# Holding the first store of a rotate kernel until nearly all loads have landed, with the last load split to make that possible

## The chip, the cores and the metric

One core of one Trainium2 chip. The metric is the device time of one execution in microseconds (us), taken over several runs; all runs in this text are in the fast state, and the granted clock is 1.00 in every profile. The change is judged against 2%. The span of a profile is 1.5 to 2 us shorter than the time of its run.

## The reference

```python
def setup_inputs():
    return {"x": np.random.randn(32, 3, 256, 256).astype(np.float32)}

def reference(x):
    return np.rot90(x, k=-1, axes=(-2, -1)).astype(np.float32)
```

96 images of 256 x 256 floats are turned by a quarter. 25.17 MB are read and 25.17 MB written. There is no arithmetic: the work is to load, transpose on VectorE, and store.

## The kernel before

The images are cut into twelve slabs of 2 MB. Each has its own SBUF tile `units[n]` of 128 partitions x 2 x 2048 floats. Slab n is turned into the tile of slab n-1, which has been consumed by then; slab 0 is turned into PSUM and copied out by ScalarE at the end.

```python
    for n in range(n_slabs):                       # all loads, on the SyncE queue
        if n == last:
            nc.sync.dma_start(out=units[n], in_=ld8_v[n])            # 2 MB, rows of 8 KB
            continue
        for i in range(I):
            if n == 0:
                nc.sync.dma_start(out=units[n][:, i], in_=ld8_v[n][:, i])
            else:                                  # 64 partitions: the even ones, then the odd ones
                nc.sync.dma_start(out=units[n][i::I].rearrange("p i f -> p (i f)"), in_=ld16_v[n, i])

    for n in range(n_slabs):
        t_in, t_out = units[n], units[n - 1] if n else turned0
        ...                                        # two VectorE transposes, t_out <- t_in
        if n == 1:                                 # first stores, same queue
            nc.sync.dma_start(out=st_v[n][:, 0, :W], in_=t_out[:, 0, :W])    # 128 KB
            nc.sync.dma_start(out=st_v[n][:, 0, W:], in_=t_out[:, 0, W:])    # 896 KB
            nc.sync.dma_start(out=st_v[n][:, 1], in_=t_out[:, 1])            # 1 MB
        elif n:
            nc.sync.dma_start(out=st_v[n], in_=t_out)                        # 2 MB
    ...                                            # ScalarE copies slab 0 out of PSUM, last store
```

Of the kernel before, what the change touches and what calls it, by code (L numbers as in the profile page):

```python
# [1 line left out]

# [4 lines left out]




@with_exitstack
def kernel(
    ctx: ExitStack,
    tc: tile.TileContext,
    x: bass.AP,
    out: bass.AP,
):

















    nc = tc.nc
    fp32 = mybir.dt.float32

    B, C, H, W = x.shape
    P = nc.NUM_PARTITIONS  # L40
    RI, RO = 16, 8
    K = H // RI
    I = 2
    Q = P // (K * I)
    n_slabs = B * C // (Q * I)
    last = n_slabs - 1
    F = RO * W

    rows_in = x.rearrange("b c h w -> (b c h) w")
    rows_out = out.rearrange("b c h w -> (b c h) w")  # L50
    ld8_v = rows_in.rearrange("(n i p r) w -> n p i (r w)", i=I, p=P, r=RO)
    ld16_v = rows_in.rearrange("(n i m r) w -> n i m (r w)", i=I, m=Q * K, r=RI)
    st_v = rows_out.rearrange("(n i p c) w -> n p i (c w)", i=I, p=P, c=RO)

    pools = [ctx.enter_context(tc.tile_pool(name=f"unit{u}", bufs=1)) for u in range(n_slabs)]
    units = [pool.tile([P, I, F], fp32, name=f"u{u}") for u, pool in enumerate(pools)]
    psum = ctx.enter_context(tc.tile_pool(name="psum", bufs=1, space=bass.MemoryType.PSUM))
    turned0 = psum.tile([P, I, F], fp32, name="turned0")

    for n in range(n_slabs):  # L60
        if n == last:
            nc.sync.dma_start(out=units[n], in_=ld8_v[n])
            continue
        for i in range(I):
            if n == 0:
                nc.sync.dma_start(out=units[n][:, i], in_=ld8_v[n][:, i])  # L66
            else:
# [4 lines that stand above are left out]
        if n in (0, last):  # L72
            for i in range(I):
                src = t_in[:, i].rearrange("p (r g c) -> p c r g", r=RO, c=RO)
                dst = t_out[:, i].rearrange("p (c g r) -> p c r g", c=RO, r=RO)
                nc.vector.transpose(out=dst[:, :, ::-1, ::-1], in_=src)  # L76
        else:
            src = t_in.rearrange("p i f -> p (i f)").rearrange("p (r g c) -> p c r g", r=RI, c=RO)
            dst = t_out.rearrange("p i (c k r) -> p c r k i", c=RO, r=RI)[:, :, ::-1, ::-1, :]
            for h in range(2):  # L80
                cs = slice(h * RO // 2, (h + 1) * RO // 2)
                nc.vector.transpose(out=dst[:, cs], in_=src[:, cs])  # L82

        if n == 1:
            nc.sync.dma_start(out=st_v[n][:, 0, :W], in_=t_out[:, 0, :W])
            nc.sync.dma_start(out=st_v[n][:, 0, W:], in_=t_out[:, 0, W:])
            nc.sync.dma_start(out=st_v[n][:, 1], in_=t_out[:, 1])
        elif n:
            nc.sync.dma_start(out=st_v[n], in_=t_out)  # L89

    for i in range(I):
        nc.scalar.copy(out=units[last][:, i], in_=turned0[:, i])  # L92
    nc.sync.dma_start(out=st_v[0], in_=units[last])


# [1 line left out]
_INS = ['x']  # L97
_OUTS = [((32, 3, 256, 256), 'float32')]


# [23 lines left out]
```

## Time and profile before

| | |
|---|---|
| time, median of 3 runs | 124.06 us (123.96 to 124.23) |
| span of the profile | 122.2 us |
| DMA engines busy | 97.8% of the span |
| VectorE busy | 93.3 us, ends at 99.2 us |
| first store issued, landed | 42.28 us, 62.93 us |

The prediction below shows the page, the windows and the timeline.

(A packet is one piece of a transfer, here 8 KB of one partition. Every transfer also has 16 completion packets of 4 bytes, 592 for the 37 transfers here. I read them as one for each of the 16 DMA engines, which tells when each was done.)

### The profile page before, as it was taken

The page shows a single profiled execution, that of the slowest core. Times are in us where ns is not written, and L with a number is a line of the kernel's source. Part 1 is how long each engine was busy: PE and PEld are TensorE (multiplying, and loading weights), DVE is VectorE, ACT ScalarE, POOL GpSimd, SP SyncE. Part 2 cuts the span into 40 slices and gives each one's busy share as a digit, 9 for nine tenths or more (in the row PEclk, how much of TensorE's full clock was granted, in tenths as well). Part 3 has the DMA queues.
Part 4 walks back from the last instruction along what each step waited for, and adds up shares of the span by engine and source line. Part 5 has one row for each costly group of instructions (what it writes and reads, how often), then busy time and mean ns, then how long its engine had stood idle before and what let it go on. Part 6 is the DMA issues. An engine that isn't in the chain of part 4 may idle for free.

```text
span 122.2 us, 134 instructions
## 1 busy us (share of the span) xinstructions
DVE 93.3 (76%) x24; ACT 5.0 (4%) x3; POOL 0.2 (0%) x4
## 2 busy tenths in 40 slices
DVE  0299999999999999999999999999999940000000
ACT  0000000000000000000040000000000651000000
POOL 0000000000000000000000000000000000000000
DMA  3999999999999999999999999999999999999993
GB/s 88 429 432 434 440 440 429 429 429 429 429 429 429 429 429 424 434 424 408 370 414 428 426 429 429 429 429 429 429 429 429 424 429 429 429 429 426 429 429 166
DMA packets 5584, 50.33 MB, mean 412 GB/s; under 512 B 592, under 2 KB 720, under 8 KB 848
## 3 DMA queue, kind: packets, MB, share of 16 engines
q1 hardware_dynamic: 5584, 50.33, 97.8%
HBM read 25.17 MB, written 25.17 MB: 412 GB/s over the span
## 4 chain that ended last, share of the span: by engine, by line
DMA 57%; DVE 13%; issue 7%; DVEq 3%; ACT 2%; SPq 1%
DMA u<-in_x_dram 39%; DMA out_dram<-u 18%; DVE u L82 10%; DVE u L76 3%; DVEq L119 3%; ACT u L92 2%; SPq L66 1%; SPq L89 0%
## 5 line engine op out<-in xcount | busy, mean ns | idle before, releaser
L82 DVE STREAM_TRANSPOSE u<-u 128x2048 f32<-128x2048 f32 x20 | 78.0, 3948 | 0.3
L76 DVE STREAM_TRANSPOSE turned<-u 128x2048 f32<-128x2048 f32 x2 | 7.6, 3828 | 5.5 <-DMA u<-in_x_dram 5.5
L76 DVE STREAM_TRANSPOSE u<-u 128x2048 f32<-128x2048 f32 x2 | 7.8, 3953 | 0.0
L92 ACT COPY u<-turned 128x2048 f32<-128x2048 f32 x2 | 3.7, 1866 | 33.8 <-DVE u L76 33.8
L92 ACT ACT_TABLE_LOAD x1 | 1.3, 1283 | 62.4 <-DMA u<-in_x_dram 62.4
L108 POOL MEMSET const-bfloat16-1.0<- 128x1 bf16 x1 | 0.1, 102 | 0.0
L108 POOL MEMSET const-uint8-127<- 128x1 uint8 x1 | 0.1, 102 | 0.0
L108 POOL MEMSET const-float32-0.0<- 128x1 f32 x1 | 0.1, 99 | 0.2 <-issue 0.2
L108 POOL MEMSET const-float32-1.0<- 128x1 f32 x1 | 0.1, 99 | 0.0
## 6 DMA issues: line engine op xcount, KB each, us to landing
u<-in_x_dram SPq DMA_DIRECT2D x22, 1024.0 KB, 19.6
out_dram<-u SPq DMA_DIRECT2D x11, 2048.0 KB, 25.0
u<-in_x_dram SPq DMA_DIRECT2D x1, 2048.0 KB, 22.5
out_dram<-u SPq DMA_DIRECT2D x1, 1024.0 KB, 20.2
out_dram<-u SPq DMA_DIRECT2D x1, 896.0 KB, 20.2
out_dram<-u SPq DMA_DIRECT2D x1, 128.0 KB, 20.6
```

The costliest lines, as they stand in the source:

```text
L66: nc.sync.dma_start(out=units[n][:, i], in_=ld8_v[n][:, i])
L76: nc.vector.transpose(out=dst[:, :, ::-1, ::-1], in_=src)
L82: nc.vector.transpose(out=dst[:, cs], in_=src[:, cs])
L92: nc.scalar.copy(out=units[last][:, i], in_=turned0[:, i])
L108: nc = _bacc.Bacc("TRN2", target_bir_lowering=False, num_devices=1)
L119: with _tile.TileContext(nc) as tc:
```

## The change

Its intent: keep stores out of the DMA queue while loads run, and leave just so many loads in flight (0.75 MB) that the latency of the first store is covered. To have something to wait on near the end, the last 2 MB load is cut in three.

```diff
+    M = P // 4
...
         if n == last:
-            nc.sync.dma_start(out=units[n], in_=ld8_v[n])
+            nc.sync.dma_start(out=units[n][:, 0], in_=ld8_v[n][:, 0])
+            near_end = nc.sync.dma_start(out=units[n][:M, 1], in_=ld8_v[n][:M, 1])
+            nc.sync.dma_start(out=units[n][M:, 1], in_=ld8_v[n][M:, 1])
             continue
...
         if n == 1:
-            nc.sync.dma_start(out=st_v[n][:, 0, :W], in_=t_out[:, 0, :W])
+            first = nc.sync.dma_start(out=st_v[n][:, 0, :W], in_=t_out[:, 0, :W])
+            tc.add_manual_dep(first.ins, near_end.ins.name, mybir.DependencyInfo(
+                mybir.DependencyClass.Sync, mybir.DependencyReason.DATA), reason="stores after loads")
```

## The prediction

> **What bounds the kernel now.** I read the page first (busy shares and the forty slices), then the chain of work that ended last, then the SyncE queue's waits and the timeline, then narrow windows and the packet records around the middle of the run, where the change acts. First the page of the kernel before:
>
> ```profile
> DVE 93.3 (76%) x24; ACT 5.0 (4%) x3; POOL 0.2 (0%) x4
> DVE  0299999999999999999999999999999940000000
> ...
> DMA  3999999999999999999999999999999999999993
> GB/s 88 429 432 434 440 440 429 429 429 429 429 429 429 429 429 424 434 424 408 370 414 428 426 429 429 429 429 429 429 429 429 424 429 429 429 429 426 429 429 166
> ...
> q1 hardware_dynamic: 5584, 50.33, 97.8%
> ...
> out_dram<-u SPq DMA_DIRECT2D x1, 128.0 KB, 20.6
> ```
>
> The 16 DMA engines are busy for 97.8% of the 122.2 us span, and the rate stands at 429 GB/s while they load and while they store. VectorE has stopped by slice 33. So bytes set the end: 50.33 MB at 429 GB/s are 117.3 us; the rest, 4.9 us, is a start of about 2.4 us, a tail of about 1.4 us after the last packet (120.83 in the packet records), and about 0.5 us lost in the one dip, slices 18 to 21 (408, 370, 414). The dip is where loads give way to stores. The windows there (columns: stretch, length, busy time of DVE, ACT and POOL, clock, DMA share, GB/s):
>
> ```profile
> 57.00:58.00 1.00, 1.00 (x1) 0.00 (x0) 0.00 (x0) 1.00 1.00 418
> 58.00:59.00 1.00, 1.00 (x1) 0.00 (x0) 0.00 (x0) 1.00 1.06 442
> 59.00:60.00 1.00, 1.00 (x1) 0.00 (x0) 0.00 (x0) 1.00 1.06 385
> 60.00:61.00 1.00, 0.96 (x2) 0.00 (x0) 0.00 (x0) 1.00 0.86 270
> 61.00:62.00 1.00, 1.00 (x1) 0.00 (x0) 0.00 (x0) 1.00 1.00 397
> 62.00:63.00 1.00, 1.00 (x1) 0.64 (x1) 0.00 (x0) 1.00 1.05 434
> ```
>
> Between 59 and 62 us the rate falls to 385, 270, 397: (429-385)+(429-270)+(429-397) = 235 KB short, or 0.55 us. The engines are not idle there. The 8 KB packets of the last load, 0.309 us each earlier on, take 0.45 to 0.77 us in some thirty cases; the first 1 KB packet of a store is recorded only at 61.36 us.
>
> The timeline shows when each store is handed to the queue (columns: start, duration, engine, line, operation):
>
> ```profile
> 1.64 36.15 SPq L68 DMA_DIRECT2D u<-in_x_dram  x20
> ...
> 13.09 78.34 DVE L82 STREAM_TRANSPOSE u<-u 128x2048 f32<-128x2048 f32 x20
> 39.77 0.39 SPq L62 DMA_DIRECT2D u<-in_x_dram  x1
> 42.28 0.36 SPq L85 DMA_DIRECT2D out_dram<-u  x1
> ...
> 101.15 0.37 SPq L93 DMA_DIRECT2D out_dram<-u  x1
> ```
>
> The first store is issued at 42.28 us but lands 20.6 us later, at 62.9: it lies behind about 8 MB of loads in the same queue. The last store is issued at 101.15 and lands at 121.18, so even there the queue has 20 us of work in hand. VectorE and ScalarE are nowhere near the path, though the printed chain follows the ScalarE copies at the end; that chain puts the time to the issue, not to the queue ahead of it.
>
> [...] each 1 MB load takes 19.56 us to land because eight lie in the queue (8 x 2.445 us)[...]. [...] the first load is issued at 0.73 us, its first packets start at 1.74 to 1.83 on eight engines and at 2.41 to 2.53 on the other eight, so 1.0 and 1.7 us; I use these. [...]
>
> **The change part by part.**
>
> 1. The last 2 MB load becomes three: 1 MB, 0.25 MB (32 partitions), 0.75 MB (96 partitions). Bytes are the same, and packets stay 8 KB. Two more issues of about 0.4 us on SyncE lie under a queue of some 8 MB: nothing on the path. Each engine gets two more completion packets of 0.009 us: 0.02 us.
>
> 2. The first store gets a second wait. The order of the issues doesn't change, as the built kernel's instruction listing confirms: all loads, then the same stores. The eight completion semaphores that the DMAs share rotate by two, so some stores wait for another predecessor; every such predecessor is a load or a store eight places earlier, done by then. In the listing the only new wait that can end last is the one on the 32-partition load.
>
> 3. The stores which used to be queued from 42 to 62 us (six issues by 57 us) are held and issued in one burst. VectorE goes on: it writes each turned slab into a buffer whose input was consumed already, and no transpose waits for a store. By 60 us slabs 1 to 5 are turned (13.09 + 7.83 us per slab puts slab 5 at 52.2 and slab 6 at 60.1), which is some 10 MB or 24 us of stores. After that a slab comes every 7.8 us and drains in 4.9, as before; the backlog at 101 us is still about 19 us. So nothing later in the run moves except by what happens at the turn.
>
> 4. The turn itself. The last 1 MB load before the final one has its per-engine completion packets at 56.21 to 56.46. The 1.25 MB ahead of the trigger are 10 packets per engine: 10 x 0.309 + 0.02 = 3.11 us, so 59.32 to 59.57; a load's semaphore counts 0.31 us after that packet (first load: packets at 4.85 to 5.11, semaphore 5.21 to 5.47): the last at about 59.9. SyncE passes a satisfied wait in 0.07 us, so the store is issued at 59.95 and its packets start 1.0 us later on half of the engines (60.95) and 1.7 us later on the other half (61.65). Meanwhile the 0.75 MB are 6 packets per engine, 1.86 us: loads end at 61.18 to 61.45. So half of the engines meet no gap, and half a gap of 0.2 to 0.45 us. The next stores follow at 0.41 us per issue; the first holds 8 packets of 0.046 us = 0.37 us per engine, so the queue doesn't run dry again by more than 0.05 us.
>
> 5. What the hold removes. Before, the loads end per engine between 61.36 and about 61.93 instead of the 61.16 to 61.41 that 16 packets of 0.309 us from 56.21 to 56.46 would give: the fastest engine lost 0.2 us, the slowest 0.5. That spread of 0.57 us is still there at the end, where the completion packets of the last store lie at 120.21 to 120.82, 0.61 us apart. The slowest engine ends the run. I suppose, without proof, that the slow load packets come from store descriptors standing right behind them. If so, the hold takes most of it away: the slowest engine goes from loads to stores at about 61.65 (its gap) instead of 61.93: -0.3 us. I count two thirds, since stores still reach half of the engines 0.2 to 0.5 us before the loads end.
>
> Sum: +0.02 (completion packets) + 0.05 (issue spacing) - 0.3 (turn), so -0.2 to -0.25: 124.06 becomes about 123.8 us.
>
> **The rivals.** (a) The wait makes a bubble: the latency is not covered by 0.75 MB. If the slow half of the engines starts 2.5 us after the landing rather than 1.7, or the landing itself is delayed because reads are slow at the turn, all of the dip (0.5) returns as idle time, and 0.5 to 1 us more: 124.3 to 125. For it: the 1.0 and 1.7 us come from one cold issue only. Against: a store reads its source from SBUF, and the first load's slow start contains an HBM read (its first packets took about 1 us instead of 0.31). (b) The slow packets belong to the end of the loads and not to the stores behind: then the dip stays and the gap partly adds: 124.1 to 124.6. For it: store packets are recorded only after the slow ones. Against: nothing like it at earlier borders between loads. (c) Reads and writes in one stretch cost much, and parting them wins over 1%: against it speaks [...] 429 GB/s on both sides of the dip; 0.55 us is all there is to win: 123.5. (d) The lost prequeueing starves the tail: against it the 20 us backlog at the last issue; even a gap of 1 us at the turn leaves VectorE and ScalarE off the path.
>
> **Range and chances.** The best case is the dip gone and no gap: 123.5; runs differ by 0.1 to 0.2 us, so the low end is 123.2. The bad case (a) gives 125 at the extreme; I put the high end at 124.7. A move of 2% is 2.5 us. On the gain side there are 0.55 us; on the loss side all engines would have to stand idle for 2.5 us in the middle, while a whole cold start takes 1.7. Hence 1% for faster, 97% for the same, 2% for slower.
>
> **What would show it.** In the changed kernel: the first store issued near 60 us in place of 42, then stores about 0.4 us apart until slab 5's; the 59 to 62 us windows at 385 or above in the first, and a dip that lies after 61 us, if at all, and shows as a low DMA share rather than slow packets; the first store landing within 3 us of its issue in place of 20.6; VectorE still ending near 99.2 and the last store still issued near 101; completion packets of the last store at 0.3 to 0.5 us apart. Step 4 is wrong if a hole of over 0.5 us with a DMA share under a half stands at 61 to 62. Step 5 is wrong if load packets of 0.45 us and over are still there before 61 us. The whole is wrong if rates away from the turn change, or if a later wait of SyncE for a store's semaphore holds a ready slab back.

+0.02, +0.05 and -0.3 us, together -0.2 to -0.25 us, are estimates from numbers of the trace. That the split adds nothing beyond its 0.02 us stands unproved.

## More of the kernel before

One more view of the kernel before is wanted for the comparison: the windows of the long store stretch (columns: stretch, its length, busy us and instructions of DVE, ACT and POOL, granted clock, share of the DMA engines, GB/s).

```profile
66.00:80.00 14.00, 13.93 (x5) 0.00 (x0) 0.00 (x0) 1.00 1.01 429
80.00:100.00 20.00, 19.16 (x5) 2.61 (x2) 0.00 (x0) 1.00 1.01 428
100.00:119.00 19.00, 0.00 (x0) 1.12 (x1) 0.00 (x0) 1.00 1.01 429
```

The rate does not move over 53 us. Behind it stands something that I looked at only after the result: in the packet records, every single 8 KB store packet from 66 to 119 us took exactly 309 ns.

## The result, and the profile after

The changed kernel takes 125.80 us in the median (125.41 to 126.25, 6 runs), the kernel before 124.09 (123.96 to 124.23, 6 runs). The ratio is 1.014, with a 95% interval of 1.0115 to 1.0165. Ratios here are the mean time of one kernel's fast runs over that of the other's from the same rounds, so not quite the ratio of the medians. It is inside the 2% band, as forecast, but on the other side of zero: 1.7 us slower, where 0.2 us faster was predicted, and outside the range. The profiled run was the slowest of the six (126.25), so the traces differ by 2.3 us of span where the medians differ by 1.7.

From the page of the changed kernel, the rate in forty slices and the issue of the first store (line, engine, operation, KB, us from issue to landing):

```profile
GB/s 90 427 453 427 427 437 432 421 437 432 421 432 432 427 427 427 442 421 395 219 357 428 429 416 429 413 424 419 421 416 421 421 421 419 421 421 421 421 421 213
...
out_dram<-u SPq DMA_DIRECT2D x1, 128.0 KB, 2.9
```

Two things have changed in the first line. The dip at slices 18 to 20 is far deeper (395, 219, 357 for 408, 370, 414). And to the right of it the rate sinks within some five slices to about 421, where it was 429, and stays there: not a stall, but a lower rate to the end. The second line shows that the wait does what it was meant to do: the first store lands 2.9 us after its issue, no longer 20.6.

The windows of the changed kernel (columns as above):

```profile
58.00:59.00 1.00, 1.00 (x1) 0.00 (x0) 0.00 (x0) 1.00 1.11 410
59.00:60.00 1.00, 1.00 (x1) 0.00 (x0) 0.00 (x0) 1.00 1.03 213
60.00:61.00 1.00, 0.96 (x2) 0.81 (x1) 0.00 (x0) 1.00 1.06 205
61.00:62.00 1.00, 1.00 (x1) 0.47 (x1) 0.00 (x0) 1.00 0.97 262
62.00:63.00 1.00, 1.00 (x1) 0.00 (x0) 0.00 (x0) 1.00 0.93 238
63.00:64.00 1.00, 1.00 (x1) 0.00 (x0) 0.00 (x0) 1.00 1.03 363
66.00:80.00 14.00, 13.93 (x5) 0.00 (x0) 0.00 (x0) 1.00 1.01 424
80.00:100.00 20.00, 19.36 (x5) 2.40 (x2) 0.00 (x0) 1.00 1.01 420
100.00:119.00 19.00, 0.00 (x0) 1.33 (x1) 0.00 (x0) 1.00 1.01 419
```

From 59 to 63 us about half the rate is missing (205 to 262 GB/s) with a DMA share of about 1 (0.93 to 1.06). So this is no idle queue: the engines are busy with packets that take long, in the packet records 0.43 to 0.76 us for every 8 KB packet in this stretch. That is not the bubble of the prediction's rival (a), which would show a low share (hold_whole below has one, of 0.06 to 0.12).

The timeline says when SyncE acted (start, duration, engine, line, operation):

```profile
42.46 0.35 SPq L65 DMA_DIRECT2D u<-in_x_dram  x1
44.91 0.32 SPq L66 DMA_DIRECT2D u<-in_x_dram  x1
...
61.84 0.37 SPq L89 DMA_DIRECT2D out_dram<-u  x1
62.30 0.38 SPq L92 DMA_DIRECT2D out_dram<-u  x1
...
101.36 0.37 SPq L99 DMA_DIRECT2D out_dram<-u  x1
```

The first store goes out at 61.84 us, not at 59.95, because the 32-partition load on which it waits (L65) landed only at 61.75. The last store is issued at 101.36, 0.2 us later than before, with 22 us of queue ahead of it: nothing in VectorE or ScalarE has become a bound.

To tell the turn from the stores I use two numbers from the landings. The third store (the 1 MB one) lands at 67.36 us before and 69.15 after: +1.8 us at the turn. From there to the last landing 53.82 us pass before and 54.44 after: +0.6 us in the store stream. Together they are the 2.4 us by which the last store lands later (123.59 for 121.18).

A landing is the last of a transfer's 16 semaphore counts (66.67 to 67.36 us for the third store before), so that of the slowest engine, and this hides part of the second loss. By the completion packets the engines end the third store 0.61 us apart before and the last store 0.61 us apart as well; after, 0.70 and then 0.26 us. In the mean of the engines, the third store ends 1.7 us later (68.28 for 66.59) and the way from there to the last store takes 0.9 us longer (54.82 for 53.90).

### The profile page after: what moved, and what is told of

Read it like the earlier page. It is cut to its first block, busy times and chain, and to the rows that moved or that the text cites. A ratio compares the mean times of both kernels' runs of the same rounds, so it can differ in the third digit from the quotient of the medians.

```text
span 124.5 us, 137 instructions
## 1 busy us (share of the span) xinstructions
DVE 93.3 (75%) x24; ACT 5.0 (4%) x3; POOL 0.2 (0%) x4
## 3 DMA queue, kind: packets, MB, share of 16 engines
q1 hardware_dynamic: 5616, 50.33, 98.1%
## 4 chain that ended last, share of the span: by engine, by line
DMA 51%; DVE 13%; issue 10%; DVEq 6%; ACT 1%
DMA u<-in_x_dram 51%; DVE u L86 13%; DVEq L125 6%; ACT u L98 1%; DVE u L80 0%
```

## The experiments

The first theory (A) after reading the trace: the 32- and 96-partition loads are slow in themselves, because of the partitions that each of them writes. That was a supposition, and why partitions should matter is shown by no trace or run here. The rival (B): the hold itself costs. Twelve kernels were run in three batches of four, each with five rounds against the kernel before on the same chip. All gave correct results. The chip differs from batch to batch, so ratios of one batch can be compared more closely than ratios of two.

A table first, to which the paragraphs refer. "Excess" is the time by which the 8 KB packets between 56 and 64 us exceeded 309 ns, summed and divided by the 16 engines. "Third store" and "to last" are the two landing numbers from above. The last column has the mean duration of the 8 KB store packets from 66 to 75 us and from 100 to 119 us. All but median and ratio are from the profiled run.

| kernel | excess, us | third store, us | to last, us | 8 KB store packet, ns | median, us | ratio to before |
|---|---|---|---|---|---|---|
| before | 0.41 | 67.36 | 53.82 | 309.0, 309.0 | 124.09 | |
| changed | 1.97 | 69.15 | 54.44 | 311.9, 315.2 | 125.80 | 1.0140 |
| split_only | 2.21 | 69.38 | 53.77 | 309.0, 309.0 | 125.72 | 1.0117 |
| hold_columns | (2 and 6 KB packets) | 68.01 | 54.99 | 318.6, 315.2 | 125.37 | 1.0095 |
| columns_only | (2 and 6 KB packets) | 68.37 | 53.80 | 309.0, 309.0 | 124.89 | 1.0054 |
| hold_whole | 0.07 | 68.81 | 54.97 | 319.7, 315.1 | 126.58 | 1.0191 |
| halves_hold | 0.07 | 66.96 | 54.73 | 311.0, 315.1 | 124.37 | 1.0019 |
| halves_only | 0.74 | 67.72 | 53.85 | 309.0, 309.0 | 124.01 | 0.9999 |
| block64_only | 2.38 | 69.39 | 53.78 | 309.0, 309.0 | 125.92 | 1.0149 |
| stride64_only | 0.37 | 67.26 | 53.85 | 309.0, 309.0 | 123.78 | 0.9972 |
| drain_mid | 0.30 | 67.15 | 56.09 | 309.0, 315.0 | 126.27 | 1.0187 |
| hold_2mb | 0.28 | 67.15 | 53.80 | 309.0, 309.0 | 123.70 | 0.9979 |
| hold_1p5mb | 0.06 | 67.03 | 53.76 | 309.0, 309.3 | 123.45 | 0.9960 |
| stride_both | 0.35 | 67.32 | 53.89 | 309.0, 309.0 | 123.95 | 0.9996 |

The kernel before had medians of 124.29, 124.06 and 123.92 us in the three batches. Measured by the 2% of this text, hold_whole and drain_mid are unclear, since their intervals reach over 1.02, and all others count as the same; what is said of smaller differences rests on their intervals. In the mean of the engines, "to last" is 53.90 us in every kernel with 309.0 ns at both places, 53.93 in hold_1p5mb, 54.68 in halves_hold, 54.82 in the changed kernel and 55.05 in hold_columns and hold_whole.

### The split without the hold (split_only)

```diff
  # against the changed kernel
-            tc.add_manual_dep(first.ins, near_end.ins.name, ...)
```

> The three-way split of the last load (128, 32 and 96 partitions) stays, the hold on the first store is taken away. Theory A (the 32- and 96-partition loads themselves run slow[...]): as slow as the changed kernel, 125.3 to 126.2 us, and windows of 200 to 270 GB/s from 59 us on, with the 8 KB load packets at 0.45 to 0.75 us. Theory B (the hold costs: the stores come late, the queue runs dry or the stores come in a burst): back to the kernel before, 123.9 to 124.3 us. Theory C (half of each): about 125.0.

Measured: 125.72 us (125.23 to 125.94), ratio 1.0117 (1.0094 to 1.014). Its windows:

```profile
59.00:60.00 1.00, 1.00 (x1) 0.00 (x0) 0.00 (x0) 1.00 1.13 229
60.00:61.00 1.00, 0.96 (x2) 0.73 (x1) 0.00 (x0) 1.00 0.97 156
61.00:62.00 1.00, 1.00 (x1) 0.56 (x1) 0.00 (x0) 1.00 0.97 238
62.00:63.00 1.00, 1.00 (x1) 0.00 (x0) 0.00 (x0) 1.00 0.90 225
...
100.00:119.00 19.00, 0.00 (x0) 1.21 (x1) 0.00 (x0) 1.00 1.01 428
```

The deep dip is there without any hold, so theory A holds for the turn: most of the loss is the split. But the store packets are back at exactly 309 ns, which means that the second loss, in the stores, comes with the hold. I had not expected that division.

### The hold with a split along the row, and its control (hold_columns, columns_only)

```diff
  # hold_columns, against the changed kernel; columns_only is the same without the hold
-            near_end = nc.sync.dma_start(out=units[n][:M, 1], in_=ld8_v[n][:M, 1])
-            nc.sync.dma_start(out=units[n][M:, 1], in_=ld8_v[n][M:, 1])
+            near_end = nc.sync.dma_start(out=units[n][:, 1, :F // 4], in_=ld8_v[n][:, 1, :F // 4])
+            nc.sync.dma_start(out=units[n][:, 1, F // 4:], in_=ld8_v[n][:, 1, F // 4:])
```

> The hold stays, at the same 0.25 MB and 0.75 MB, but the last megabyte is split along the row (128 partitions x 2 KB, then 128 x 6 KB) and no longer by partitions. Theory A: the loads run at full rate up to the turn; 123.5 to 124.4 us, and the prediction's sum for the hold (-0.2 us) gets its first clean test. Theory B: as slow as the changed kernel, 125.3 to 126.2 us.

> The control of the run before it: the column split, no hold. Theories A and B both expect the kernel before within 0.2 us (123.9 to 124.3). If it is slower by 0.5 us or more, one more split of any kind costs[...].

Measured: 125.37 us with the hold (ratio 1.0095, 1.0074 to 1.0115) and 124.89 without (1.0054, 1.0036 to 1.0073). Both are misses. The control is 0.6 us slower than the kernel before, so this was not a clean way to split: its 2 KB packets took 0.08 us at best and up to 0.73 us, while the 6 KB packets behind them ran at 0.234 us, the rate of the 8 KB ones. All 128 partitions take part, so theory A doesn't explain it. The stores behind explain part: with the stores held, the same packets took 0.38 us at most, and their sum per engine was 1.19 us for 1.60, where 8 packets at 0.084 are 0.67. The rest I did not follow further. By my own words of expectation one more split of any kind costs, which left theory A in doubt, and it needed a better test (below).

The pair is still of use, as the hold is the only difference within it. With the hold the third store lands 0.36 us earlier (68.01 for 68.37), which has the sign and about the size of the saving at the turn that the prediction counted on, and then the stores take 1.2 us longer (54.99 for 53.80) with packets of 315 ns and more. A saving and a larger loss.

### The last load whole, all stores held until it has landed (hold_whole)

```diff
  # against the kernel before
-            nc.sync.dma_start(out=units[n], in_=ld8_v[n])
+            near_end = nc.sync.dma_start(out=units[n], in_=ld8_v[n])
...
+        for st in held if n else []:      # every store of slabs 1 to 11
+            tc.add_manual_dep(st.ins, near_end.ins.name, ...)
```

> The last load is left whole, and every store is held until it has landed: no store descriptor is in the queue while loads run. If the slow load packets of 59 to 61 us come from stores right behind the loads (step 5 of the prediction), they are gone here (8 KB packets all under 0.33 us, windows at 420 to 440 until 61 us), then an idle gap of about 0.3 (landing) + 0.1 + 1.0 to 1.7 us follows: 124.9 to 125.5 us in all. If they belong to the end of the loads, the dip to 270 GB/s stays and the gap comes on top: 125.4 to 126.0.

Measured: 126.58 us, ratio 1.0191 (1.0169 to 1.0212), some 1.1 us above what was expected. Its windows:

```profile
59.00:60.00 1.00, 1.00 (x1) 0.00 (x0) 0.00 (x0) 1.00 1.04 434
60.00:61.00 1.00, 0.96 (x2) 0.00 (x0) 0.00 (x0) 1.00 0.89 369
61.00:62.00 1.00, 1.00 (x1) 0.00 (x0) 0.00 (x0) 1.00 0.12 49
62.00:63.00 1.00, 1.00 (x1) 0.95 (x1) 0.00 (x0) 1.00 0.06 23
```

Here the share is low together with the rate: this is what an empty queue looks like. No load packet exceeded 0.33 us (excess 0.07 us for 0.41). So one supposition of the prediction is confirmed in this kernel: with no stores behind the loads, the slow load packets of the dip are gone. (hold_1p5mb below adds a condition: stores that had stood there for only about 2 us did no such harm, with 0.06 us of excess.) The records also give the latency of a store into an empty queue: issued at 62.05 us, first packets on the engines at 62.90, all within some 0.15 us, so 0.85 us and not the 1.0 and 1.7 us that I took from the first load. The 1.1 us above expectation are the slower stores (54.97 for 53.82).

### Whole halves, with and without the hold (halves_hold, halves_only)

```diff
  # halves_hold, against the changed kernel; halves_only is the same without the hold
             near_end = nc.sync.dma_start(out=units[n][:, 0], in_=ld8_v[n][:, 0])
-            ... [:M, 1] and [M:, 1]
+            nc.sync.dma_start(out=units[n][:, 1], in_=ld8_v[n][:, 1])
```

> The last load is split into its two full 1 MB halves (128 partitions x 8 KB each) and the first store is held until the first half has landed, so 1 MB is left in flight. The loads use whole rows and all partitions. Theory so far, from the first four runs: the partition split costs 1.8 to 2.0 us at the turn; the hold itself saves about 0.3 us at the turn, but in all three kernels with a hold the 8 KB store packets took 315 ns on average in place of 309, which costs about 1.1 us over the stores. It expects no dip at 59 to 61 us, 315 ns packets after it, and 124.6 to 125.0 us. Rival (the slow stores come from the queue having run dry, and with 1 MB in flight it doesn't): 309 ns packets and 123.6 to 124.0 us.

> Control of the run before it: the two halves, no hold. The kernel before within 0.2 us (124.0 to 124.4), store packets of 309 ns, the dip at 59 to 61 us as before. If it is 0.5 us slower, a split of any kind costs[...].

Measured: 124.37 us with the hold (ratio 1.0019, 1.0006 to 1.0033), 124.01 without (0.9999, 0.9981 to 1.0018). The control is as fast as the kernel before, so a split by itself need not cost anything, though in its profiled run the dip was deeper (0.74 us of excess for 0.41). With the hold the dip is gone and the third store lands at 66.96 us, 0.40 us earlier than in the kernel before and 0.76 us earlier than in the control. The time is between the two expectations, and the packets say why: 80% of them were at exactly 309 ns from 66 to 75 us, 29% from 90 to 100 us, 11% from 100 to 119 us. The stores start clean and wear out. This made me suspect that the 309 ns are a state which can get lost; drain_mid below tests it.

### Which partitions, or how many (block64_only, stride64_only)

```diff
  # no hold in either; block64_only, then stride64_only
-            ... units[n][:M, 1] and units[n][M:, 1], M = 32
+            ... units[n][:64, 1] and units[n][64:, 1]
+            ... units[n][0::2, 1] and units[n][1::2, 1]
```

> No hold; the last megabyte is split into partitions 0 to 63 and 64 to 127. [...] both run at half rate: 2.45 us more than the 2.45 us of a full-rate megabyte: packets near 0.62 us throughout and 126.5 to 127.0 us, slower than the 32/96 split[...]. Rival (a DMA of fewer partitions is slow whichever they are, or one more DMA at the end costs): like the 32/96 split, about 125.7.

> No hold; the last megabyte is split into the even and the odd partitions, 64 each as in the run before it[...]. [...] full rate, 124.0 to 124.6 us. Rival (fewer partitions are slow as such): as slow as the run before it.

In both texts the figures before the word "Rival" are those of theory A. For the half rate there is a measured ground: the 32- and 96-partition loads of the changed kernel ran at 205 to 262 GB/s from 59 to 63 us, for 428 GB/s from 3 to 59 us.

Measured: 125.92 us in blocks (ratio 1.0149, 1.0134 to 1.0163) and 123.78 us interleaved (0.9972, 0.9959 to 0.9985). Two windows of the blocks, then of the interleaved parts:

```profile
60.00:61.00 1.00, 0.96 (x2) 0.80 (x1) 0.00 (x0) 1.00 1.13 238
61.00:62.00 1.00, 1.00 (x1) 0.49 (x1) 0.00 (x0) 1.00 0.91 205
```

```profile
59.00:60.00 1.00, 1.00 (x1) 0.45 (x1) 0.00 (x0) 1.00 1.05 426
60.00:61.00 1.00, 0.96 (x2) 0.84 (x1) 0.00 (x0) 1.00 1.00 320
```

Same bytes, same number of DMAs, same number of partitions, same row length; only which partitions go together differs, and 2.1 us lie between them. That tells which partitions from how many: 64 partitions in a block ran at about half rate (205 and 238 GB/s in these windows; nine in ten packets of 0.56 to 0.65 us, for 0.309), the 64 even ones at full rate (426 GB/s) until the usual dip. Why a block is slow is not shown.

The rows that are read from memory go along with the partitions, which would be a rival: a block reads 0.5 MB in one piece, the even partitions read every second row. But the kernel before had answered it. Its 20 loads of slabs 1 to 10 each bring 1 MB in one piece to the 64 even or the 64 odd partitions, and from 3 to 56 us they ran at 430 GB/s. So neither 64 partitions nor one piece of memory made these loads slow, and the profile that the prediction read showed it.

The interleaved kernel is 0.2 us below its expectation. The block's time was 0.6 us under its own, and taken alone it would have fitted the rival. The likely reason for the miss: I added the half-rate loss of 2.45 us to a run that kept the 0.41 us dip, while slow loads take the place of that dip. 2.45 - 0.41 = 2.0 us is what the trace shows at the third store (69.39 for 67.36).

### Emptying the queue in the middle of the stores (drain_mid)

```diff
  # against the kernel before
+            st = nc.sync.dma_start(out=st_v[n], in_=t_out)
+            if n == 5:
+                drain = st
+            if n > 5:                     # and the last store as well
+                tc.add_manual_dep(st.ins, drain.ins.name, ...)
```

> The kernel before, no hold at the turn, but every store from the seventh slab on waits until the store of the slab before has landed (at about 87 us), so that the queue runs empty once in the middle of the stores and 14 MB follow. Theory S (the 309 ns store packets are a state that the engines bring along from stores waiting behind the loads, and lose when the queue restarts from empty): exactly 309 ns until 87 us, about 315 ns on average after it, 1.9 us of gap (as with the last load held whole) + 0.6 us for the slower 14 MB: 126.4 to 126.8 us. Rival (the slow stores come from the hold's burst of waiting stores at the turn, or are tied to the turn in another way): 309 ns after the gap too, 125.8 to 126.2 us.

Measured: 126.27 us (ratio 1.0187, 1.017 to 1.0204), 0.1 us below the expectation and 0.1 us above the rival's, so the time doesn't decide. The packets do. The windows of the gap and after it:

```profile
86.00:87.00 1.00, 1.00 (x1) 0.00 (x0) 0.00 (x0) 1.00 0.04 16
...
100.00:119.00 19.00, 0.00 (x0) 1.19 (x1) 0.00 (x0) 1.00 1.01 420
```

All 8 KB store packets from 66 to 80 us took 309 ns; after the gap the mean was 315.7 (90 to 100 us) and 315.0 ns (100 to 119 us). There is no hold at the turn in this kernel, and the turn was 25 us earlier. So neither the turn nor the split is needed to lose the 309 ns: here it was enough that the queue ran empty (a DMA share of 0.04 from 86 to 87 us) and restarted. The restart was a burst here as well (four stores issued from 86.76 to 88.79 us), so this run alone does not part the empty queue from the burst; the next two do.

### More in flight when the hold opens (hold_2mb, hold_1p5mb)

```diff
  # against hold_whole: hold_2mb waits on the load before the last one
-            near_end = nc.sync.dma_start(out=units[n], in_=ld8_v[n])
+            nc.sync.dma_start(out=units[n], in_=ld8_v[n])
...
-                nc.sync.dma_start(out=units[n][i::I]...)
+                near_end = nc.sync.dma_start(out=units[n][i::I]...)
  # hold_1p5mb waits on the even partitions of the last slab's first half
+            near_end = nc.sync.dma_start(out=units[n][0::2, 0], in_=ld8_v[n][0::2, 0])
+            nc.sync.dma_start(out=units[n][1::2, 0], in_=ld8_v[n][1::2, 0])
+            nc.sync.dma_start(out=units[n][:, 1], in_=ld8_v[n][:, 1])
```

> The last load whole; all stores held until the load before it has landed, so that 2 MB are in flight and the stores enter the queue some 3 us before the loads end; then they come in the same burst as in the other kernels with a hold. Theory S: stores stand behind the loads again, so the dip at 59 to 61 us is back, and the store packets are at 309 ns to the end: the kernel before within 0.2 us (123.9 to 124.3). Rival (the hold as such, or its burst, slows the stores): 315 ns and 124.7 to 125.2 us.

> As the run before it, with 1.5 MB in flight: the last load as even partitions and odd partitions of its first megabyte, then the whole second one, the stores held for the first of these. Between the hold with 1 MB (no dip, 309 ns at first and 315 ns from 100 us) and that with 2 MB. Theory S: part of the dip is back and the stores stay at 309 ns longer or to the end; 123.7 to 124.3 us. If there is no dip and 309 ns to the end, it is the best of both: 123.4 to 123.7.

Measured: 123.70 us (ratio 0.9979, 0.9966 to 0.9992) and 123.45 us (0.9960, 0.9947 to 0.9973). Windows of the second:

```profile
60.00:61.00 1.00, 0.96 (x2) 0.93 (x1) 0.00 (x0) 1.00 1.04 434
61.00:62.00 1.00, 1.00 (x1) 0.00 (x0) 0.00 (x0) 1.00 1.01 390
...
100.00:119.00 19.00, 0.00 (x0) 1.26 (x1) 0.00 (x0) 1.00 1.01 428
```

hold_2mb is 0.2 us below its expectation. hold_1p5mb missed the first of its two expectations (there is no dip) and met the second.

Both kernels issue their stores in the same burst after a hold as the changed kernel does, and have 309 ns packets. So it is neither the hold as such nor the burst that slows the stores. What orders the kernels with a hold is how long the stores stand in the queue before the loads run out. With the 0.85 us from issue to the engines, an estimate of that lead is (negative: the engines had run out of loads before the stores came):

| kernel | first store issued | loads end on the engines | lead, us | stores | dip |
|---|---|---|---|---|---|
| hold_whole | 62.05 | 60.7 to 61.5 | -2.2 to -1.4 | 320, then 315 ns | none |
| hold_columns | 60.93 | 61.6 to 62.2 | -0.2 to 0.4 | 319, then 315 ns | (2 KB packets) |
| changed | 61.84 | 62.8 to 63.6 | 0.1 to 0.9 | 312, then 315 ns | (slow split) |
| halves_hold | 59.55 | 61.0 to 61.5 | 0.6 to 1.1 | 311, then 315 ns | none |
| hold_1p5mb | 58.41 | 61.1 to 61.6 | 1.8 to 2.3 | 309 ns, 309.3 at the end | none |
| hold_2mb | 57.09 | 61.2 to 61.7 | 3.3 to 3.8 | 309 ns | partly back (0.28 us) |

Without a hold the stores stand there for 14 us or more, with 309 ns and a dip of 0.3 to 0.7 us. In these kernels more stores wait the longer the lead is, so whether the time or the number counts is not told. One rival can be set aside: that the engines lose rate when they start in step. At the third store they are as far apart in halves_hold (0.45 us) as in hold_1p5mb (0.48 us).

The hold with 1.5 MB in flight has the best of both, and beats both kernels: 0.4% faster than the kernel before. How much of that is owed to its interleaved pieces is not shown, since it has no control without the hold; stride64_only has such pieces, no hold, and was 0.28% faster.

### Interleaving the whole last load (stride_both)

```diff
  # against the kernel before
-            nc.sync.dma_start(out=units[n], in_=ld8_v[n])
+            nc.sync.dma_start(out=units[n][0::2], in_=ld8_v[n][0::2])
+            nc.sync.dma_start(out=units[n][1::2], in_=ld8_v[n][1::2])
```

> No hold; the whole last load is split into its even and its odd partitions (64 x 16 KB each), as the run that split only the last megabyte that way was 0.28% faster than the kernel before. If interleaved partitions at the turn shorten the dip: 123.6 to 123.9 us, 309 ns store packets. If that run owed its gain to the smaller last pieces (0.5 MB): the kernel before, 124.0 to 124.3.

Measured: 123.95 us, ratio 0.9996 (0.998 to 1.0013): the kernel before. So interleaving as such gains nothing, and the 0.28% of stride64_only may have to do with its last pieces of 0.5 MB. That is not shown.

## Why the prediction was wrong

The view of what bounds the kernel stood the test: bytes on the DMA engines (97.8% busy before, 98.1% after), VectorE and ScalarE off the path, no later wait that holds a ready slab back. So did the class, within 2%; but a loss of 1.4% came near that limit, by ways that the prediction had not booked, so this hit says little for its reasoning. The size and the sign did not hold.

- **Step 1, the split of the last load, is the main failure.** It was booked at 0.02 us, for completion packets alone; that it costs no data time was assumed, and no trace showed it. Alone, it costs 1.2% (split_only, 1.4 us), and its 8 KB packets had an excess of 2.21 us per engine for 0.41. The blocks and the interleaved halves (2.38 and 0.37 us of excess) show that the cause is which partitions go together. How the 1.8 us by which the excess grew follow from the 32 and the 96 partitions is not shown.
- **Step 2**, the waits, was right: the wait on the 32-partition load ends last (16.5 us of SyncE's waits at L89), and no other new one matters.
- **Step 3** said that nothing later in the run moves "except by what happens at the turn". This is the second failure. The stores of the changed kernel run at 315 ns in place of 309 per 8 KB, which comes to +0.9 us in the mean of its engines (+0.6 by the last landing) and to 0.8 to 1.2 us in the other kernels with a short lead. What was missing: the steady 429 GB/s of the stores depends on what the queue went through before (420 GB/s after the gap of drain_mid), and a hold can lose it (419 from 100 to 119 us in the changed kernel).
- **Step 4**, the timing of the turn, fell with step 1. The trigger landed at 61.75 and not at 59.9 us. About half of this came after the last packet: the completion packets of the 32-partition load end at 60.52 us and not at 59.57, and the last semaphore count follows 1.2 us after that and not 0.31 (0.36 by the first load's own numbers). The latency it took for the store was too long: 0.85 us on all engines, not 1.0 and 1.7. The gap it feared on half of the engines did not come: at 0.75 MB the first store packets follow the loads at once (62.84 us). An empty queue shows only in hold_whole and drain_mid (DMA shares of 0.06 and 0.04), and for some 0.2 us on half of the engines in hold_columns.
- **Step 5**, what the hold removes, was right in sign and about right in size: -0.3 us was counted, and the hold moved the third store by -0.36 us within the column pair, by -0.76 us within the halves pair and by -0.40 us from the kernel before to halves_hold. That the slow load packets of the dip go away when no stores stand behind is shown by hold_whole (0.07 us of excess); that this is not all is shown by hold_1p5mb (0.06 us, with stores behind).
- **Of the rivals**, none was the true one. (a) came nearest. It allowed for a landing delayed by slow reads, which came true, but it booked the loss as idle time, and the DMA share of about 1 in the dip speaks against that. (b) is refuted by hold_whole. (d) looked for a starved tail and not for a slow one.
- **Small slips in its readings**, which change nothing in the sum: seven stores and not six were issued by 57 us (the seventh at 56.95); 20 load packets took 0.45 us or more, up to 0.78, and some thirty took over 0.33; and the three parts of the 4.9 us outside the steady rate add up to 4.3.

For the changed kernel, split and hold are not simply added: its trace has, by the landings, +1.8 us at the turn (split_only +2.0) and +0.6 us in the stores, and its time ratio is 1.0140 for 1.0117 of the split alone. These two ratios come from different batches and their intervals touch, so the hold's own share in the unprofiled time of the changed kernel is not settled; in the column pair and the halves pair, each from one batch, it is about 0.4 and 0.2% (in the halves pair the intervals overlap too). The traces show how a loss can stay small: in the mean of the engines the two kernels end the third store together (68.28 and 68.30 us), then the stores of the changed kernel lose 0.9 us; but its engines end 0.26 us apart and those of split_only 1.10, so at the slowest engine, which ends the run, only 0.45 us are left (123.26 for 122.81).

What stays open: why stores that have stood behind loads run at 309 ns per packet. The runs show only how that is lost: bit by bit in halves_hold (80% of the packets at 309 ns from 66 to 75 us, 11% from 100 to 119 us), from 112 us on in hold_1p5mb (309.3 ns in the mean of 100 to 119 us), and by 90 us after the restart from empty in drain_mid (315.7 ns). Open too is why a block of partitions loads slowly, why 128 short rows of 2 KB load slowly even with the stores held (up to 0.38 us a packet, for 0.08 at best), and why stores that have stood behind the loads for about 2 us do not slow them yet.

## What to carry to other kernels

When a DMA is cut by partitions, cut it so that each part still spreads over all of them (every second one, not a block); here blocks of 64, and a block of 32 followed by its 96, ran at about half the rate (156 to 262 GB/s from 59 to 63 us, where the even partitions had 426 until 60 us), and a high DMA share with half the GB/s was the mark. A hold that keeps two streams apart had to open early enough here that the next transfers were in the queue well before the last ones ended: a lead of 1.8 to 2.3 us was right, one of 0.6 to 1.1 us cost rate for the rest of the run (420 GB/s from 100 to 119 us, for 428), and one of over 3 us brought back part of the dip (0.28 us of excess, for 0.06). And where a rate is flat, look at the single packets before taking the rate for granted: a line of identical durations (309 ns here, 315 on average after) can be a state that a change breaks.
